# Two paced queues of woven work in the mixers of a two-layer decoder trunk, with four smaller edits

## The chip, the cores and the metric

The kernel runs on one core of a Trainium2 chip. The metric is the device time of one execution in microseconds (us); the time before is the median of 3 runs. The engines are TensorE (PE; its weight loads are PEld), VectorE (DVE), ScalarE (ACT), GpSimd (POOL) and SyncE (SP), which issues the loads.

## The reference

The input is 512 tokens of width 1024, with 16 learned tokens put in front, so 528 columns. There are two layers, and in float32 each layer computes

```python
h = h + rmsnorm(mixer(rmsnorm(h, pre_mix)), post_mix)
h = h + rmsnorm(conv_ffn(rmsnorm(h, pre_ffn)), post_ffn)
```

The mixer is one projection of 1024 to 3600 columns, split into: queries, keys, values and gates of four *retention* heads (rq, rk, rv, rg; 128 wide, rotary on rq and rk, a fixed decay per head); queries, keys, values and gates of four *gated* heads (gq, gk 64 wide, gv, gr 128 wide); and a rank-16 input ga, from which the gated heads' decays come as `log_sigmoid(ga @ w2 + b) / 16`, one per token and key. Retention heads end in a norm with mean and variance, gated heads in a norm with the mean square alone; both are multiplied by silu of their gates, put side by side and sent through one output projection. The second half of a layer is a gated MLP of width 2816 with a causal convolution of three taps between the up-projection and `gelu(a) * g`.

## The kernel before, in words

Activations lie with channels on partitions and tokens along the free dimension. Every large product is done with three float16 matmuls (high x high, low x high, high x low) into one bank: `product_step`, L386 to L388. A weight block of 1024 x 128 is loaded by SP into a stage buffer (st); ScalarE makes its float16 high half (L109), VectorE the low half (L110). The result is a *unit*; there are 10 unit buffers. Tokens are done in two halves (columns 0 to 232 and 232 to 528), so a projection tile is two *half tiles* of 24 matmuls (16 for ga).

**The mixer** (`mixer`, L884) projects 29 tiles in the order of `TILES`. The first LEAD tiles do their first halves, then their second halves, as the second half of the normalised input is not ready before; layer 1 finishes that norm (`self.later`) at this point. All further tiles do both halves in a row. After each half tile comes `tick(2)`, which takes two steps of woven work.

**Woven work** is written as Python generators that yield between steps. `vtr` turns a v tile (2 steps). `gla(pr)` does a pair of gated heads: the decay (`gla_decay`, 3 steps), the diagonal scores (1), eight level steps (`gla_scores`, L833 to L884: each makes a float16 pair lvx with L867 on ScalarE and L868 on VectorE, multiplies k on GpSimd (L870) and q on VectorE (L872), and does the previous level's matmuls lps at L818, merged by predicated copies at L827), the turned k, the states (2), and `head_out`. `ret(h)` does one retention head: scores and turned k (2), states (2), `head_out`. `head_out` (L659) makes the outputs o and o2 in PSUM, one bank each per head; takes statistics on VectorE (L686, L687); forms the reciprocal root with a power on GpSimd (L320); scales into on (L706 for retention, L708 for gated heads); waits until the head's gate is projected; and then, for two token ranges, transposes (pto, L718), multiplies by the gate (L721) and splits into the float16 pair merged (L324, L325). A generator whose gate or v is missing yields "waits" and the next one in the list is tried.

All generators stand in one list, `self.bg`. A step goes to the first that doesn't wait, with `vtr` put at the head of the list, so work runs nearly in series: pair 0 of the gated heads, pair 1, then the retention heads, with the gated heads' last steps when their gates come. Before, all eight gates are the last eight tiles, gr first.

**Order of instructions.** Outside a first region whose order is given by hand, what Python traces is only a ranking. A planner with its own cost model then sets the order on each engine: of the instructions that it believes ready, the earliest traced goes first. `keep_in_program_order` pins an instruction behind everything traced before it on its engine. On the chip each engine works through that fixed order. PSUM has two pools: three banks for projections (`mm`) and five for everything else (`mx`).

**The last stage** (`last_down`, L1133, and `Quarter`, L116) does the last down-projection over quarters of the weight matrix with seven products (w11, t1, t2, w22, t3, w21, t4), five of them on sums of quarters. `Quarter.fetch` traces a load, an addition on VectorE (L143) that adds the landed quarter to one kept, the high half on ScalarE (L154) and the low half on VectorE (L157), up to 8 blocks ahead of use. The loads are pinned, and the high halves of w11 and t1; the additions are not. After w11 and t1, ScalarE copies the sums out (part, L1160) and t2 goes into the same banks. Results (yo, L1168) free banks in which the residual is transposed (hp, L1189).

**The output projection** (`out_proj`, L988) contracts the eight heads in the order 4, 5, 6, 7, 0, 1, 2, 3, where 0 to 3 are retention and 4 to 7 gated heads.

Of the kernel before, what the change touches and what calls it, by code (L numbers as in the profile page):

```python
# [9 lines left out]
F32 = mybir.dt.float32  # L10
# [28 lines left out]
TICK = 2  # L39
# [4 lines left out]
LEAD = (9, 10)  # L44
# [10 lines left out]
TILES += [(nm, 2 * i + j) for i in range(2) for nm in ("rk", "rq", "rv") for j in range(2)]  # L55
TILES += [(nm, h) for nm in ("gr", "rg") for h in range(4)]
# [10 lines left out]
MIXKINDS = (("vnt", P, 6), ("mv", 20, 4), ("bst", 6, 8), ("ms", 10, 4), ("ont", P, 8), ("dgrt", 16, 4), ("dgt", 32, 2))  # L67
# [48 lines left out]
class Quarter:  # L116
# [22 lines left out]
    def fetch(self):  # L139
# [3 lines left out]
        add = lambda to, x: nc.vector.tensor_tensor(out=to, in0=to, in1=x, op=ALU.add)  # L143
# [16 lines left out]
class Kern:  # L160
    def __init__(self, ctx, tc, a):
# [13 lines left out]
        self.rate = 1  # L175
# [6 lines left out]
    def tick(self, n=1):  # L182
        for _ in range(n):
            i = 0
            while i < len(self.bg):
                try:
                    if next(self.bg[i]) is None:
                        break
                    i += 1
                except StopIteration:  # L190
                    self.bg.pop(i)
# [8 lines left out]
    def drain(self):  # L200
        while self.bg:
            self.tick(TICK)

# [171 lines left out]
    def product(self, ps, units, rhs, n0, n1):  # L375

        tot = len(units)
        for i, ((w, kk), x) in enumerate(zip(units, rhs)):
            self.product_step(ps, w, kk, x, n0, n1, i == 0, i == tot - 1)
            if i % 8 == 7 and i + 1 < tot:  # L380
                self.tick(self.rate)
# [277 lines left out]
    def head_out(self, heads):  # L659
# [20 lines left out]
        mv = self.sm([P, n, 5, 2], "mv")  # L680
        nc.gpsimd.memset(mv[:, :, 4, :], 1.0)
        for h in range(n):
            for i in range(5):
                wi = CHUNKS[i][1]
                st = self.sm([P, 6], "bst")
                nc.vector.bn_stats(out=st[:wi], in_=src(h, i))  # L686
                nc.vector.bn_aggr(out=mv[:wi, h, i, :], in_=st[:wi])  # L687
        ret = heads[0][-1] is not None
        if ret:
            r = self.rstd(mv[:, 0, :, 1], 5, 1.0, self.decay[:, 1, heads[0][-1], :])  # L690
# [6 lines left out]
        onvs = []  # L697
        for h in range(n):
            on, ont = self.g([P, 4, P], F32, "on"), self.sm([16, P], "ont")
            onvs.append((on, ont))  # L700
# [584 lines left out]
```

## Time and profile before

| | |
|---|---|
| time, median of 3 runs | 1280.14 us (1280.01 to 1281.91) |
| the profiled execution | 1280.94 us |
| its span, first to last instruction | 1279.2 us |
| mean granted TensorE clock | 0.996 |
| TensorE busy | 1238.6 us (97%) |
| VectorE, ScalarE, GpSimd busy | 827.5, 640.8, 161.5 us |

By the timeline the first mixer runs to about 241 us and the second from 652 to about 878 us; the last stage begins near 1163 us. In a row of groups the columns are: line, engine, operation, what it writes and reads with shapes, count, then busy time and mean ns of one, then the engine's idle time just before and what ended it. Mean ns of a matmul is its latency; matmuls overlap, so the busy time of groups on PE can't be added up. In a row of waits the columns are total us, times and longest. In a timeline row the first two numbers are the start in the span and the duration.

### The profile page before, as it was taken

To read this page: it belongs to the slowest core of one execution; us is meant where nothing else is said; L and a number is where in the kernel's file an instruction comes from. 1 tells how busy PE (TensorE), PEld (TensorE's weight loads), DVE (VectorE), ACT (ScalarE), POOL (GpSimd) and SP (SyncE) were. 2 spreads that over 40 slices of the span, in tenths; PEclk is the share of its full clock that TensorE was granted. 3 is DMA by queue.
4 is the path that set the end of the run, shared out by engine and by line. 5 is a ranking of instruction groups with operands and counts; after the bars stand their busy time and mean duration, and the time that the engine had idled before them with its cause. 6 is when DMAs were issued, how large, how long until landed. Compare 5 with 4: busy or idle time off the path is not lost.

```text
span 1279.2 us, 26402 instructions
## 1 busy us (share of the span) xinstructions
PE 1238.6 (97%) x11106; PEld 1018.2 (80%) x11106; DVE 827.5 (65%) x1518; ACT 640.8 (50%) x1194; POOL 161.5 (13%) x206
## 2 busy tenths in 40 slices
PE   8999999999999999999999898999999999999997
PEld 7877788989888888988887776788898888885443
DVE  5567855467876666422476768454579768887865
ACT  5664443354855555422346544343548656664541
POOL 1013310152000000000330223101530000000000
PEclk9999999999999999999999999999999999999999
DMA  7932212131533323223143321121315333306551
GB/s 208 254 98 68 67 50 83 51 98 35 155 105 95 97 89 91 74 79 97 50 117 96 102 69 51 50 67 50 99 35 159 106 100 100 116 2 201 170 180 66
DMA packets 206828, 124.18 MB, mean 97 GB/s; under 512 B 6689, under 2 KB 194133, under 8 KB 206709
## 3 DMA queue, kind: packets, MB, share of 16 engines
q1 hardware_dynamic: 206548, 121.97, 32.6%
q8 instruction: 87, 1.43, 0.5%
q0 software_dynamic: 160, 0.52, 0.1%
q14 instruction: 33, 0.26, 0.1%
HBM read 120.38 MB, written 2.10 MB: 96 GB/s over the span
## 4 chain that ended last, share of the span: by engine, by line
PE 79%; DVE 9%; ACT 4%; DMA 3%; issue 2%; POOL 2%; SPq 0%; DVEq 0%; POOLq 0%; ACTq 0%
PE pu L387 12%; PE pu L388 12%; PE pu L386 12%; PE pj L386 6%; PE pj L388 6%; PE pj L387 6%; PE pl L1150 3%; PE pd L386 3%; PE pd L388 3%; PE pd L387 3%; DMA st<-in_ffn_down 2%; DVE unit L110 2%; PE po L386 1%; PE po L387 1%; PE po L388 1%
## 5 line engine op out<-in xcount | busy, mean ns | idle before, releaser
L387 PE MATMUL pu<-every,unit 128*128 128x296 f16 (+2 forms) x1408 | 385.4, 274 | 2.1 <-DVE every L325 2.1
L388 PE MATMUL pu<-every,unit 128*128 128x296 f16 (+2 forms) x1408 | 385.4, 274 | 0.0
L386 PE MATMUL pu<-every,unit 128*128 128x296 f16 (+2 forms) x1408 | 383.7, 274 | 0.8 <-ACT every L324 0.7
L110 DVE SCALAR_TENSOR_TENSOR unit<-st,unit 128x1024 f16<-128x1024 f32 x184 | 228.2, 1240 | 162.6 <-ACT unit L109 160.1
L386 PEld LDWEIGHTS <-unit 128*128 128x128 f16 x2912 | 285.4, 98 | 51.0 <-issue 7.0
L388 PEld LDWEIGHTS <-unit 128*128 128x128 f16 x2912 | 285.4, 98 | 46.4 <-issue 3.3
L387 PEld LDWEIGHTS <-unit 128*128 128x128 f16 x2912 | 285.7, 98 | 42.2 <-issue 0.5
L109 ACT ACTIVATE unit<-st 128x1024 f16<-128x1024 f32 x184 | 191.4, 1041 | 134.7 <-PE pu L388 52.7
L386 PE MATMUL pj<-every,unit 128*128 128x296 f16 (+2 forms) x896 | 247.3, 276 | 1.4 <-DVE room L831 1.0
L388 PE MATMUL pj<-every,unit 128*128 128x296 f16 (+2 forms) x896 | 246.8, 276 | 0.7 <-DVE unit L110 0.7
L387 PE MATMUL pj<-every,unit 128*128 128x296 f16 (+2 forms) x896 | 247.3, 276 | 0.0
L1035 ACT ACTIVATE u<-pu 128x296 f32<-128x296 f32 (+2 forms) x176 | 66.3, 379 | 95.9 <-PE pu L388 95.7
L388 PE MATMUL pd<-av,unit 128*128 128x232 f16 (+1 forms) x352 | 96.9, 276 | 0.0
L387 PE MATMUL pd<-av,unit 128*128 128x296 f16 (+1 forms) x352 | 96.8, 276 | 0.0
L386 PE MATMUL pd<-av,unit 128*128 128x232 f16 (+1 forms) x352 | 96.7, 276 | 0.0
L352 DVE TENSOR_TENSOR acc<-acc,sq 128x296 f32<-128x296 f32 (+2 forms) x60 | 33.3, 556 | 75.1 <-ACT sq L350 73.2
L320 POOL TENSOR_TENSOR every<-every 128x1 f32<-128x1 f32 (+5 forms) x33 | 38.8, 1177 | 298.5 <-DVE every L317 124.4
L1150 PE MATMUL pl<-unit,fk 128*128 128x512 f16 x330 | 73.2, 385 | 2.5 <-ACT part L1160 2.5
L386 PE MATMUL po<-merged,unit 128*128 128x296 f16 (+2 forms) x256 | 69.6, 274 | 0.7 <-ACT merged L324 0.7
L387 PE MATMUL po<-merged,unit 128*128 128x296 f16 (+2 forms) x256 | 70.0, 274 | 0.0
L1024 DVE SCALAR_TENSOR_TENSOR cg<-u,every,cg 128x527 f32<-128x527 f32 (+1 forms) x88 | 66.5, 755 | 5.5 <-ACT cg L1019 4.3
L388 PE MATMUL po<-merged,unit 128*128 128x296 f16 (+2 forms) x256 | 70.0, 274 | 0.0
(221 smaller groups left out, 1521.7 us busy)
## 6 DMA issues: line engine op xcount, KB each, us to landing
st<-in_ffn_up SPq DMA_DIRECT2D x88, 512.0 KB, 3.8
st<-in_w_in SPq DMA_DIRECT2D x56, 512.0 KB, 4.1
st<-in_ffn_down SPq DMA_DIRECT2D x46, 512.0 KB, 4.2
st<-in_w_out SPq DMA_DIRECT2D x16, 512.0 KB, 3.5
st<-in_ffn_down SPq DMA_DIRECT2D x8, 384.0 KB, 2.9
out<-yo SPq DMA_DIRECT2D x8, 256.0 KB, 2.0
xt<-in_x SPq DMA_DIRECT2D x6, 256.0 KB, 6.4
w<-in_ffn_down SPq DMA_DIRECT2D x3, 512.0 KB
```

The costliest lines, as they stand in the source:

```text
L109: nc.scalar.activation(u[:, 0], st, AF.Copy, scale=SW)
L110: nc.vector.scalar_tensor_tensor(out=u[:, 1], in0=st, scalar=SW, in1=u[:, 0], op0=ALU.mult, op1=ALU.subtract)
L320: nc.gpsimd.tensor_tensor(out=r[:w, :n], in0=t[:w, :n], in1=self.mhalf[:w, :n], op=ALU.pow)
L352: eng.tensor_tensor(out=acc[:, :n], in0=acc[:, :n], in1=sq[:, :n], op=ALU.add)
L386: nc.tensor.matmul(ps[:, :n], w[:, 0, kk, :], x[:, 0, n0:n1], start=first, stop=False)
L387: nc.tensor.matmul(ps[:, :n], w[:, 0, kk, :], x[:, 1, n0:n1], start=False, stop=False)
L388: nc.tensor.matmul(ps[:, :n], w[:, 1, kk, :], x[:, 0, n0:n1], start=False, stop=last)
L1024: nc.vector.scalar_tensor_tensor(out=to, in0=u[:, max(lo, d) - d : L - d], scalar=self.cvec[:, ci(i) : ci(i) + 1], in1=to, op0=ALU.mult, o ...
L1035: nc.scalar.activation(u[:, n0:n1], ps[:, : n1 - n0], AF.Copy, scale=IXW)
L1150: mm = lambda x, w, **kw: nc.tensor.matmul(ps, x, w, skip_group_check=more, **kw)
```

## The change

1. *Two queues with a pace.* The pairs of gated heads go to a list of their own, `self.gated`; everything else stays in `self.bg`, now strictly in order of arrival (`vtr` no longer at the head). After each half tile `advance` gives each queue one credit (at most one is kept), and takes steps while there is credit. A step costs 0.7; a level step yields `LEVEL / PACE[0]` and so costs 1.5. `tick` is left for the other stages, with one step a call as they had it.
2. *Tiles.* The gates gr 0 and gr 1 come right after the first two retention heads' tiles, gr 2 and gr 3 last of all. The leading tiles of layer 1 are nine where they were ten.
3. *Norms of gated heads.* ScalarE squares each output chunk with a running sum and later scales it; the statistics, the square of the mean and the scaling on VectorE go for these heads. Retention heads keep theirs.
4. *Output projection.* Heads are contracted in the order 0, 1, 4, 5, 2, 3, 6, 7.
5. *Last stage.* The additions of `Quarter.fetch` are pinned in program order.

```diff
-TICK = 2
+PACE = (0.7, 0.7)
+LEVEL = 1.5
-LEAD = (9, 10)
+LEAD = (9, 9)
-TILES += [(nm, 2 * i + j) for i in range(2) for nm in ("rk", "rq", "rv") for j in range(2)]
-TILES += [(nm, h) for nm in ("gr", "rg") for h in range(4)]
+TILES += [(nm, j) for nm in ("rk", "rq", "rv") for j in range(2)] + [("gr", 0), ("gr", 1)]
+TILES += [(nm, j) for nm in ("rk", "rq", "rv") for j in range(2, 4)] + [("rg", h) for h in range(4)] + [("gr", 2), ("gr", 3)]
...
-        add = lambda to, x: nc.vector.tensor_tensor(out=to, in0=to, in1=x, op=ALU.add)
+        add = lambda to, x: kern.tc.keep_in_program_order(nc.vector.tensor_tensor(out=to, in0=to, in1=x, op=ALU.add))
...
+    def step(self, queue):
+        i = 0
+        while i < len(queue):
+            try:
+                n = next(queue[i])
+                if n != "waits":
+                    return n or 1.0
+                i += 1
+            except StopIteration:
+                queue.pop(i)
+        return 0
+    def tick(self):
+        self.step(self.bg)
+    def advance(self):
+        for i, queue in enumerate((self.gated, self.bg)):
+            self.credit[i] = min(self.credit[i] + 1.0, 1.0)
+            while self.credit[i] > 0:
+                n = self.step(queue)
+                if not n:
+                    break
+                self.credit[i] -= n * PACE[i]
...
     def drain(self):
-        while self.bg:
-            self.tick(TICK)
+        while self.bg or self.gated:
+            for queue in (self.gated, self.bg):
+                self.step(queue)
...
         yield
-        mv = self.sm([P, n, 5, 2], "mv")
...
+        ret = heads[0][-1] is not None
+        onvs = [(self.g([P, 4, P], F32, "on"), self.sm([16, P], "ont")) for _ in heads]
+        if ret:
...
         else:
             q = self.sm([P, n, 5], "ms")
-            nc.vector.tensor_tensor(out=q, in0=mv[:, :, :, 0], in1=mv[:, :, :, 0], op=ALU.mult)
-            nc.vector.tensor_tensor(out=q, in0=q, in1=mv[:, :, :, 1], op=ALU.add)
-            r = self.rstd(q.rearrange("p h i -> p (h i)"), 5 * n, 1.0, EPS * 64.0)
-        yield
+            nc.gpsimd.memset(q[:, :, 4], 1.0)
+            for h, i, wi in each:
+                nc.scalar.activation(to(h, i), src(h, i), AF.Square, accum_out=q[:wi, h, i : i + 1])
+            r = self.rstd(q.rearrange("p h i -> p (h i)"), 5 * n, 1.0 / P, EPS * 64.0)
+        yield
...
+                nc.scalar.activation(to(h, i), src(h, i), AF.Copy, scale=rr)
...
-            yield
+            yield LEVEL / PACE[0]
...
-                self.spawn(gla(0))
-                self.spawn(gla(1))
+                self.gated.extend([gla(0), gla(1)])
             elif nm in ("gv", "rv"):
-                self.bg.insert(0, vtr((nm, h)))
+                self.spawn(vtr((nm, h)))
...
-            self.tick(TICK)
-        self.rate = 1
+            self.advance()
...
-        order = [4, 5, 6, 7, 0, 1, 2, 3]
+        order = [0, 1, 4, 5, 2, 3, 6, 7]
```

More of the change, by code (lines that the diff above doesn't have):

```diff
@@ L174, in __init__ @@
         self.bg = []
-        self.rate = 1
+        self.gated, self.credit = [], [0.0, 0.0]
         self.rings = {}
@@ L180, in spawn @@
         self.bg.append(gen)
[L182 to L191, printed above, removed]
+    def step(self, queue):
[19 more added lines that the diff above has]
+                self.credit[i] -= n * PACE[i]
     def finish(self, gen):
@@ L380, in product @@
             if i % 8 == 7 and i + 1 < tot:
[L381 removed]
+                self.tick()
     def product_step(self, ps, w, kk, x, n0, n1, first, last):
@@ L679, in head_out @@
         yield
-        mv = self.sm([P, n, 5, 2], "mv")
[L681 to L684, printed above, removed]
+        ret = heads[0][-1] is not None
+        onvs = [(self.g([P, 4, P], F32, "on"), self.sm([16, P], "ont")) for _ in heads]
+        to = lambda h, i: onvs[h][0][:, i, :] if i < 4 else onvs[h][1]
+        each = [(h, i, CHUNKS[i][1]) for h in range(n) for i in range(5)]
+        if ret:
+            mv = self.sm([P, 5, 2], "mv")
+            nc.gpsimd.memset(mv[:, 4, :], 1.0)
+            for h, i, wi in each:
@@ L685, in head_out @@
                 st = self.sm([P, 6], "bst")
                 nc.vector.bn_stats(out=st[:wi], in_=src(h, i))
[L687 to L690, printed above, removed]
+                nc.vector.bn_aggr(out=mv[:wi, i, :], in_=st[:wi])
+            r = self.rstd(mv[:, :, 1], 5, 1.0, self.decay[:, 1, heads[0][-1], :])
         else:
             q = self.sm([P, n, 5], "ms")
-            nc.vector.tensor_tensor(out=q, in0=mv[:, :, :, 0], in1=mv[:, :, :, 0], op=ALU.mult)
-            nc.vector.tensor_tensor(out=q, in0=q, in1=mv[:, :, :, 1], op=ALU.add)
-            r = self.rstd(q.rearrange("p h i -> p (h i)"), 5 * n, 1.0, EPS * 64.0)
+            nc.gpsimd.memset(q[:, :, 4], 1.0)
@@ L696, in head_out @@
+            for h, i, wi in each:
+                nc.scalar.activation(to(h, i), src(h, i), AF.Square, accum_out=q[:wi, h, i : i + 1])
+            r = self.rstd(q.rearrange("p h i -> p (h i)"), 5 * n, 1.0 / P, EPS * 64.0)
         yield
[L697 to L700, printed above, removed]
-            for i in range(5):
-                wi = CHUNKS[i][1]
-                to = on[:, i, :] if i < 4 else ont
-                rr = r[:wi, 5 * h + i : 5 * h + i + 1]
-                if ret:
-                    nc.vector.tensor_scalar(out=to, in0=src(h, i), scalar1=mv[:wi, h, i, 0:1], scalar2=rr, op0=ALU.subtract, op1=ALU.mult)
-                else:
-                    nc.vector.tensor_scalar(out=to, in0=src(h, i), scalar1=rr, scalar2=None, op0=ALU.mult)
+        for h, i, wi in each:
+            rr = r[:wi, 5 * h + i : 5 * h + i + 1]
+            if ret:
+                nc.vector.tensor_scalar(out=to(h, i), in0=src(h, i), scalar1=mv[:wi, i, 0:1], scalar2=rr, op0=ALU.subtract, op1=ALU.mult)
+            else:
+                nc.scalar.activation(to(h, i), src(h, i), AF.Copy, scale=rr)
```

4 lines of the change are left out of this document (1 added, 3 removed).

## The prediction

> **What bounds the kernel now.** I read the page first, then the busy time by stretch, then the list of waits.
>
> ```profile
> PE 1238.6 (97%) x11106; PEld 1018.2 (80%) x11106; DVE 827.5 (65%) x1518; ACT 640.8 (50%) x1194; POOL 161.5 (13%) x206
> ```
>
> TensorE works for 1238.6 of 1279.2 us, and the change takes no matmul away. What can be won is its idle time, 40.6 us, and time at a lowered clock. Some of the idle time is the start and the last 7 us, which the change doesn't touch. So the question is how much lies in the two mixers. By stretch (span, then PE, PEld, DVE, ACT and POOL busy, clock, DMA):
>
> ```profile
> 75.00:155.00 80.00, 74.63 (x967) 59.10 (x965) 65.83 (x168) 39.90 (x77) 26.14 (x28) 1.00 0.24 69
> 710.00:812.00 102.00, 90.10 (x1083) 70.89 (x1082) 77.78 (x211) 44.40 (x86) 29.20 (x38) 0.98 0.22 63
> 155.00:245.00 90.00, 89.77 (x780) 77.75 (x779) 50.63 (x154) 36.22 (x84) 9.97 (x10) 1.00 0.22 64
> ```
>
> The reader is to see that the idle time has a place. In 75 to 155 and 710 to 812, where the gated heads' level scores are worked, PE loses 5.4 and 11.9 us, and VectorE is busy 82% and 76% of the time. In 155 to 245, where the retention heads run, PE loses 0.2 us. This row also gives the cost of a projection matmul: 89.77 us for 780 is 115 ns, so a half tile of 24 takes 2.8 us.
>
> ```profile
> PE lps L818 <- ACT lvx L867: 9.3, 14, 1.6
> PE lps L818 <- DVE lvx L868: 2.9, 3, 1.2
> PE pl L1150 <- ACT part L1160: 2.5, 1, 2.5
> ...
> PE pto L718 <- DVE on L706: 1.5, 1, 1.5
> PE hp L1189 <- DVE yo L1168: 1.3, 1, 1.3
> PE rst L743 <- DVE on L708: 1.1, 1, 1.1
> PE ptv L637 <- ACT room L646: 1.0, 1, 1.0
> ```
>
> These are waits of PE over the whole span. The level scores (lps) wait 12.2 us for their split operand (lvx). Three more lie in the last stage and at the mixer's end (pl, pto, hp: 5.3 us). The last two rows are matmuls that waited for a bank of the five-bank pool to be read out.
>
> **Part 1: the pace.** One level is a chain: ACT makes the high half, VectorE the low half, GpSimd multiplies k, and the next level starts.
>
> ```profile
> L867 ACT ACTIVATE lvx<-room 128x528 f16<-128x528 f32 x16 | 11.5, 717 | 25.2 <-DVE room L872 12.4 <-DVE room L853 5.1 <-DVE tots L875 4.0
> ```
>
> ```profile
> L868 DVE TENSOR_TENSOR lvx<-room,lvx 128x528 f16<-128x528 f32 x16 | 11.8, 736 | 2.3 <-ACT lvx L867 2.0
> ```
>
> ```profile
> L870 POOL TENSOR_TENSOR room<-room,tots 128x264 f32<-128x264 f32 x12 | 10.6, 883 | 13.1 <-DVE lvx L868 10.9 <-DVE tots L875 2.1
> ```
>
> ```profile
> L818 PE MATMUL lps<-lvx x192: 162/190/200, 84.3 to 108.5; 64*128 64x64 f16 x168, 64*16 64x8 f16 x24
> ```
>
> ```profile
> 88.30 0.20 PE L818 MATMUL lps<-lvx 64*128 64x64 f16 x2 [1.41 <-ACT lvx L867]
> ```
>
> Alone the chain takes 0.72 + 0.74 + 0.88 = 2.3 us; as it ran, seven levels from 84.3 to 108.5, one level took 24.2 / 6 = 4.0 us, since the three engines do other work between. The code before asks for two steps after each half tile, a level in 1.4 us of projections. That can't be kept, so the planner fills PE with later projections and puts each lps where its own costs say that lvx is just ready. There is no slack, and where the chip is later than the planner thinks, PE stands (the 1.41 us at 88.30). After the change a level is charged 1.5 half tiles, 4.1 us of projections, with lps and the second queue's matmuls on top: by working the two queues through by hand, the first pair's levels fall after half tiles 15 to 26 of the sequence (before: 19 to 22) and the second pair's after 36 to 47 (before: 28 to 33): 24 half tiles have a level among them instead of 10. The pace asked, 4.1 us plus the woven rest, is at or above the 4.0 us that the chain took, so lps comes up in PE's order after lvx is done.
>
> Removed: of the 17.3 us idle in the two stretches, those that end on lvx (12.2) and most of what goes with them. Bounds: 0 (the planner still leaves no slack) to 17.3. I take 13.0, three quarters, as the pace clears the chain by little and VectorE, at 82%, still is the fullest engine behind PE there.
>
> **Part 2: the gated norms on ScalarE.** For a pair of heads VectorE's 10 statistics, 10 aggregates, 2 small operations and 10 scalings go, and ScalarE gets 10 squares with a sum and 10 scaled copies.
>
> ```profile
> L686 DVE BATCH_NORM_STATS2 room<-o x10: 253/278/299, 115.8 to 118.1; 128x6 f32<-128x128 f32 x8, 16x6 f32<-16x128 f32 x2
> L708 DVE TENSOR_SCALAR on<-o,every x8: 329/335/350, 121.3 to 123.3; 128x128 f32<-128x128 f32 x8
> ```
>
> ```profile
> L645 ACT ACTIVATE vn<-ptv,every 128x128 f32<-128x128 f32 x32 | 9.0, 364 | 7.2 <-PE ptv L637 7.2
> L758 ACT ACTIVATE sn<-kv 128x128 f32<-128x128 f32 x32 | 8.9, 277 | 26.4 <-PE kv L757 26.0
> ...
> L905 ACT ACT_TABLE_LOAD x2 | 2.6, 1283 | 0.0
> ...
> L1170 ACT ACTIVATION_READ_ACCUMULATOR sqo<-yo 128x1 f32 x6 | 1.1, 186 | 0.0
> ```
>
> ```profile
> L320 POOL TENSOR_TENSOR every<-every 128x10 f32<-128x10 f32 x4 | 7.9, 1965 | 0.5
> ```
>
> No row shows a square of 128x128 with a sum; nearest are a PSUM copy (277 ns) and the read of a sum (186 ns): 10 x 0.46 = 4.6 us, and 10 copies with a scale per partition at 0.36 = 3.6 us. ScalarE gets 8.2 us a pair, 33 us in all, and goes from 641 to 674 us, 53% of the span; VectorE loses some 6 us a pair. Neither lies on PE's path while projections run. What does: a pair's four o banks of the pool of five. Now they are held from 115.8 (first statistic) to about 123.7, 8 us; after, 4.6 + 2.0 (the power on GpSimd) + 3.6 and two hand-overs make 10 to 11 us. Who waits behind: the transposes of v, scores and outputs of the retention queue, each wanting one or two banks, and now issued beside the gated queue rather than after it. Bounds: 0 (three projection banks cover 3 x 2.8 = 8.4 us) to 4 pairs x 2.5 = 10 us. I take +2.5, as the two rows of bank waits above are 1 us each.
>
> The gates gr 0 and gr 1 come between the two pairs' exponentials (a, L801), so the Silu table is loaded, the exponential's again, and Silu again: two more loads a mixer, 4 x 1.28 = 5.1 us on ScalarE, beside half-idle time. The Trainium skill's "ScalarE: Activation LUTs", under "Rules for kernel authors", speaks against this: do all of one table set before switching. By its figure of 2.66 us a switch, drain included, the four would be 10.6 us; by the row they are 5.1, and on PE's path nothing by either while ScalarE is half idle.
>
> **Part 3: nine leading tiles, the gates' place, the order of the output projection.** In layer 1 the second halves start one half tile sooner, but their input comes from a chain of its own:
>
> ```profile
> 673.94 0.82 PE L546 MATMUL nbc<-ndg,every 99*128 99x99 f32 x6
> ```
>
> ```profile
> 674.79 1.82 DVE L559 SCALAR_TENSOR_TENSOR tmp<-every,nbc 128x296 f32<-128x296 f32 x4 [2.33 <-PE nbc L546]
> ```
>
> The first operand of the second half appears only after 674.8. If PE arrives a half tile, 2.8 us, earlier it can stand up to 2.8 us, or nothing if the planner draws the tenth tile's first half forward. I take +0.7.
>
> At the end of a mixer the output projection now contracts heads in the order in which they come ready. Before, layer 1 ended with PE waiting 1.5 us for the last retention norm (pto above), and then came these steps:
>
> ```profile
> 888.07 0.40 DVE tmp L721
> 888.55 0.42 ACT merged L324
> ```
>
> After, by the same hand count, what is left for the end is one step of the second gated pair, its norm done five half tiles before. After the last gate: Silu, product, high and low half, four steps of some 0.4 us by these rows, 1.7 us, lie under 7 heads x 3 matmuls x 0.115 = 2.4 us. So the 1.5 us go in layer 1. Bounds 0 and -1.5; I take -1.5, since its cause, the late norm, is gone.
>
> **Part 4: ordered sums.** In the last stage VectorE adds landing weight quarters (L143), and ScalarE (L154) makes their high halves:
>
> ```profile
> 1173.42 1.23 DVE L143 TENSOR_TENSOR w<-w,st 128x1024 f32<-128x1024 f32 x1 [1.76 <-DMA st<-in_ffn_down]
> ...
> 1179.10 2.35 DVE L143 TENSOR_TENSOR every<-every,st 128x1024 f32<-128x1024 f32 x2
> ```
>
> ```profile
> 1193.03 2.03 ACT L1160 ACTIVATE part<-pl 128x512 f32<-128x512 f32 x4
> ```
>
> The sums on w at 1173.42 and after belong to the next product (t2), the one at 1179.10 to the product that is running (t1, quarter 8), whose data was asked for first. t1's high halves keep their order on ScalarE, so t2's queue up behind them, and the copy of the first sums (part) comes at 1193.03; PE stands 2.5 us for it. With sums in program order t1's come first, the high halves start some 6 us sooner (1179.1 - 1173.4), and ScalarE is free when PE is done. SP's loads stand in the same order and wait for the buffers that the sums give back, so they come no later. Likewise the sums of the last product (t4) now follow the results that free the banks for hp: 1.3 us. Bounds: a gain of 3.8; a loss of 2.4, if a sum of t4 and its low half, 1.2 us each, now come late for PE, since an ordered sum that waits for its DMA holds all of VectorE behind it. I take -3.0, near the two rows of waits.
>
> **Part 5: the clock.** The stretches before and in each fall of the clock:
>
> ```profile
> 784.00:788.00 4.00, 1.59 (x51) 1.17 (x51) 4.00 (x11) 1.26 (x3) 0.67 (x2) 1.00 0.44 131
> 788.00:792.00 4.00, 4.00 (x20) 2.34 (x17) 2.58 (x5) 1.35 (x4) 2.26 (x4) 0.57 0.00 0
> ...
> 1190.00:1194.00 4.00, 1.53 (x8) 0.63 (x7) 4.00 (x5) 4.00 (x7) 0.00 (x0) 1.00 0.46 161
> 1194.00:1198.00 4.00, 4.00 (x13) 1.47 (x11) 3.01 (x4) 1.92 (x4) 0.00 (x0) 0.57 0.00 0
> ```
>
> Twice, right after PE had been idle for 2.4 to 2.5 of 4 us, the granted clock was 0.57 over 4 us, which costs 0.43 x 4 = 1.7 us. Both stalls are ones that parts 1 and 4 should end. Bounds 0 to -3.4; I take -1.7, as other stretches may now be the idle ones. The Trainium skill's "TensorE: Matmul & The Clock Gate", under "HAM oscillation", has the clock fall after gaps over about 3.4 us. By that rule these shorter waits would not be the cause, nothing would be won here, and the sum below would end at 1266.6. The trace's waits are 2.5 us at most, so it doesn't agree.
>
> **The sum.** -13.0 + 2.5 + 0.7 - 1.5 - 3.0 - 1.7 = -16.0 us. The profiled execution took 1280.94 us, 1279.2 of it span and 1.7 around it, and lies 0.8 above the median of 1280.14: 1280.94 - 16.0 = 1264.9 us, which I forecast as 1265. With the best bounds (-17.3, 0, 0, -1.5, -3.8, -3.4) it is 1255; with the worst (0, +10, +2.8, 0, +2.4, 0) 1296.
>
> **The rivals.**
>
> *The planner leaves no slack at any pace.* Then the waits on lvx stay and move with the levels; of the sum 13.0 go, and half of the clock's 1.7: -2.2, so 1278.8. For it: the planner ranks by its own costs, and these costs stay as they are. Against it: 155 to 245, where the same planner weaves at the same two steps a half tile with shorter chains, has 0.2 us of idle time.
>
> *The banks become the bound, and the kernel slower.* Two queues now want the five-bank pool at once. By the hand count the first gated pair's outputs (four banks) and those of retention head 0 (two) are issued after the same half tile, 29; the second pair's share half tile 50 with the transposes of the last v. Where such a matmul stands next in PE's order, the three projection banks are no cover, and PE waits for what is left of 10.5 us. It decides from the point where the wait exceeds some 2.5 us at two matmuls for each of the four pairs: at that price 8 x 2.5 = 20 in place of the 2.5 taken, and as late retention work pushes the levels, half of the 13.0 goes: -16.0 + 17.5 + 6.5 = +8.0, so 1289. For it: rst and ptv already waited for banks. Against it: four banks are held for 8 us now too, and cost 1 us.
>
> *The second gated pair comes late.* Its queue has little to spare: 8 levels at 1.5 and 13 steps at 0.7 make 21.1 half tiles a pair, 42.2 of the 45 there are. If it lags by the three half tiles that lie between its norm and the end beyond the 10.5 us, each output projection waits for the norm instead of for a gate. At 4 us a mixer, and without the 1.5 of part 3: -16.0 + 1.5 + 8.0 = -6.5, so 1274. For it: level chains run late by nature. Against it: VectorE is relieved just there.
>
> **How the numbers follow.** The forecast has 0.60, no slack 0.14, the banks 0.15, the late pair 0.11. Anything within 0.2% (2.6 us, 1277.6 to 1282.7) can't be told from no change here. Faster: nearly all of the first, most of the late pair and a third of the no-slack case, 0.72; no change: mostly no slack, 0.10; slower: the banks and the rest, 0.18. The forecast's own range is 1255 to 1273 (the better bounds, and half of the worse ones); for 8 in 10 it reaches on to the late pair and the no-slack case and leaves most of the banks' out: 1254 to 1284, the lower end 1 us under the best bounds for the idle time that has no row.
>
> **What would show it.** Right: waits of lps on lvx under 4 us in all where they were 12.2; PE idle in the two mixers' level stretches under 6 us; no wait for part, and none of pto in layer 1; ScalarE near 674 us with four more table loads; no 0.57 stretch in the second mixer. Wrong: new rows of PE waiting for on, vn or sn (banks), long waits before po (late pair), or lps rows as before (no slack).

## The result and the profile after

The changed kernel took 1273.3 us (median of 4 runs, 1272.95 to 1275.55) against 1281.03 us for the kernel before on the same chip: a ratio of 0.9943, with a 95% interval of 0.9926 to 0.996. That is 7.7 us faster. The forecast was 1265 us, 16.0 us faster. The sign was right and under half of the size came.

The profiled execution took 1275.55 us, with a span of 1273.8 us (before: 1279.2). Its page has this row:

```profile
PE 1239.0 (97%) x11106; PEld 1022.0 (80%) x11106; DVE 802.6 (63%) x1390; ACT 666.4 (52%) x1318; POOL 163.0 (13%) x206
```

TensorE's idle time fell from 40.6 to 34.8 us; its busy time did not fall. By stage (span, then PE, PEld, DVE, ACT and POOL busy, granted clock, DMA), before and then after; the stretches are the first mixer, its output projection, the second mixer, its output projection, and the last stage. The two feed-forward parts left out are as long as they were.

```profile
0.00:241.50 241.50, 231.55 (x2279) 193.68 (x2279) 153.80 (x387) 122.09 (x250) 41.78 (x56) 1.00 0.40 114
241.50:288.30 46.80, 45.93 (x408) 39.68 (x407) 25.60 (x45) 22.35 (x51) 21.88 (x23) 1.00 0.28 80
...
651.70:877.70 226.00, 213.53 (x2167) 177.76 (x2167) 146.81 (x371) 106.51 (x223) 44.05 (x59) 0.99 0.27 78
877.70:927.50 49.80, 47.40 (x419) 40.13 (x419) 23.92 (x53) 21.91 (x52) 19.51 (x23) 1.00 0.26 75
...
1162.50:1279.20 116.70, 105.64 (x496) 49.04 (x494) 80.68 (x96) 44.84 (x63) 3.25 (x6) 0.97 0.51 167
```

```profile
0.00:239.50 239.50, 230.30 (x2262) 193.72 (x2263) 138.03 (x307) 132.55 (x304) 39.40 (x56) 0.99 0.40 115
239.50:290.90 51.40, 48.65 (x424) 41.43 (x423) 29.30 (x61) 24.78 (x57) 22.04 (x23) 1.00 0.25 72
...
654.40:876.70 222.30, 214.27 (x2161) 179.47 (x2161) 130.88 (x299) 116.21 (x279) 46.05 (x56) 0.97 0.28 79
876.70:927.10 50.40, 47.72 (x425) 40.60 (x424) 26.61 (x61) 24.37 (x57) 19.71 (x24) 1.00 0.25 74
...
1162.10:1273.80 111.70, 103.40 (x496) 48.81 (x494) 81.05 (x96) 45.26 (x63) 4.75 (x6) 0.98 0.51 174
```

Added up per layer, the first mixer with its output projection became 2.6 us longer (288.3 to 290.9), the second 3.1 us shorter (275.8 to 272.7), the last stage 5.0 us shorter. The first mixer alone ended 2.0 us sooner; its output projection, which now also holds 424 matmuls where it had 408, took 4.6 us more.

The waits of PE after (total us, times, longest):

```profile
PE lps L831 <- ACT lvx L880: 3.6, 2, 1.9
PE rs L755 <- POOL rq L746: 2.8, 2, 1.8
PE pto L731 <- DVE on L719: 2.7, 2, 1.4
PE pu L404 <- DVE every L342: 2.1, 4, 0.6
PE ptv L654 <- ACT gv L918: 2.0, 1, 2.0
...
PE pj L403 <- DVE on L719: 1.7, 2, 0.9
PE po L403 <- DVE tmp L734: 1.5, 2, 0.9
```

The 12.2 us on lvx are 3.6 now, and part and hp are gone. In their place stand waits that are new or longer: the retention scores (rs) for the rope's sum on GpSimd and a value tile's transposes (ptv) for that tile's own copy out of its bank are new; the last transposes (pto) now wait for a retention head's norm in both mixers, where they waited in one; and po waits for the merged product (tmp).

The second part is the clock. In the trace the granted clock is either full or half, and half in stretches of 3.413 us or twice that. Before there were two such stretches ahead of the last matmul, at 788.2 and 1194.4 us (6.8 us at half clock). After there are five windows, at 170.6, 655.3, 706.5 and two from 805.5 (17.1 us). Windows of the kernel after, each dip with the window ahead of it:

```profile
167.20:170.60 3.40, 1.66 (x37) 1.35 (x37) 3.40 (x8) 1.57 (x4) 1.59 (x2) 1.00 0.01 2
170.60:174.00 3.40, 3.40 (x16) 2.11 (x15) 3.28 (x9) 0.09 (x1) 1.92 (x2) 0.50 0.53 154
```

```profile
651.90:655.30 3.40, 1.19 (x10) 0.74 (x9) 3.39 (x8) 2.63 (x7) 0.34 (x8) 1.00 0.42 120
655.30:658.70 3.40, 3.35 (x18) 2.56 (x18) 3.40 (x11) 1.74 (x5) 0.00 (x0) 0.50 1.14 309
703.10:706.50 3.40, 1.35 (x16) 0.98 (x16) 1.50 (x2) 3.37 (x7) 0.00 (x0) 1.00 0.48 139
706.50:709.90 3.40, 3.40 (x23) 2.06 (x22) 2.56 (x6) 0.62 (x3) 0.00 (x0) 0.50 0.71 201
802.10:805.50 3.40, 1.53 (x37) 0.88 (x34) 3.40 (x7) 2.25 (x4) 3.08 (x3) 1.00 0.00 0
805.50:812.30 6.80, 5.05 (x22) 3.25 (x21) 4.66 (x13) 0.64 (x1) 4.47 (x5) 0.50 0.27 80
```

Ahead of each fall PE was busy for 1.19 to 1.66 us of a window, 35 to 49%. If a half-clock window cost half its length, the clock's share would have gone from 3.4 to 8.5 us in these two profiled executions, 5.1 us against the change. The timed executions give a smaller price and a smaller share. The kernel after, with its repeat below, had eight: the four at a mean clock of 0.996 took 1272.95 to 1273.2 us, the three at 0.992 took 1274.9 to 1275.55, so about 2.3 us for a difference of some three windows. Over all kernels measured here, a mean clock lower by 0.001 goes with about 0.7 us from one execution of a kernel to the next; a half-clock window takes off 0.0013, so it costs some 0.9 us by this estimate. And the kernel before had a mean clock of 0.9948 in the 52 executions that were timed beside the experiments, the kernel after 0.9943: of the difference of their medians the clock carries about 0.4 us, not 5.1. The experiments test the waits and the clock.

### The profile page after: what moved, and what is told of

The parts are those of the page before. It is cut to its first block, busy times and chain, and to the rows that moved or that the text cites. A ratio compares the mean times of both kernels' runs of the same rounds, so it can differ in the third digit from the quotient of the medians.

```text
span 1273.8 us, 26361 instructions
## 1 busy us (share of the span) xinstructions
PE 1239.0 (97%) x11106; PEld 1022.0 (80%) x11106; DVE 802.6 (63%) x1390; ACT 666.4 (52%) x1318; POOL 163.0 (13%) x206
## 4 chain that ended last, share of the span: by engine, by line
PE 82%; DVE 5%; ACT 4%; issue 4%; POOL 2%; DMA 1%; SPq 1%; POOLq 0%; DVEq 0%; ACTq 0%
PE pu L404 12%; PE pu L405 12%; PE pu L403 12%; PE pl L1160 8%; PE pj L403 6%; PE pj L405 6%; PE pj L404 6%; PE pd L403 3%; PE pd L405 3%; PE pd L404 3%; DVE unit L111 1%; PE po L404 1%; PE po L405 1%; ACT unit L110 1%; PE po L403 1%
## 5 line engine op out<-in xcount | busy, mean ns | idle before, releaser
L337 POOL TENSOR_TENSOR every<-every 128x1 f32<-128x1 f32 (+5 forms) x33 | 41.4, 1256 | 326.3 <-DVE every L336 235.1
```

Source lines behind the costliest of these rows:

```text
L337: nc.gpsimd.tensor_tensor(out=r[:w, :n], in0=t[:w, :n], in1=self.mhalf[:w, :n], op=ALU.pow)
```

## The experiments

Medians are compared with the kernel before as timed beside them on the same chip (1280.1, 1279.9, 1279.6 and 1281.0 us). The kernel after had 1273.3 and, repeated, 1273.95; "1273.6" in the expectations is their mean.

### The last stage and the mixers, each alone

The first kernel is the one before with `add` pinned, the second the one after with `add` free.

```diff
-        add = lambda to, x: nc.vector.tensor_tensor(out=to, in0=to, in1=x, op=ALU.add)
+        add = lambda to, x: kern.tc.keep_in_program_order(nc.vector.tensor_tensor(out=to, in0=to, in1=x, op=ALU.add))
```

> The kernel before with the one edit of the last stage alone: the adds of the sums stay in program order. My theory after the two traces: the last stage became 5.0 us shorter by this edit alone, 3.3 us of it the waits that went (part, hp) and 1.7 us the half-clock stretch at 1194 us that followed such a wait. So about 1281.0 - 5.0 = 1276.0 us (1275 to 1278), and the last stage shows no wait of TensorE on part or hp. Rival: the half-clock stretch is chance and the idle time comes back elsewhere; then not over 1.7 us are gained, 1279.3 us or more.

> The kernel after without the ordered sums, so with all that was changed in the mixers. My theory: the mixers are worth 7.7 - 5.0 = 2.7 us, since the 8.6 us that the waits on lvx lose are taken back by new stalls (ret scores behind the rope sum on GpSimd, values behind gv, merged tiles at the end) and by more half-clock stretches: 1278.3 us (1277 to 1280). Rival: the sums are worth 1.7 us or less, and the mixers 6: 1275 us.

Measured: sums alone 1279.15 us (ratio 0.9991, 0.9979 to 1.0002), mixers alone 1274.67 us (0.9952, 0.9938 to 0.9966). My attribution fell: the mixers carry some 5.4 us and the sums about 1, which the interval of the sums alone does not tell from nothing. The last stage of each, sums alone and then mixers alone:

```profile
1164.00:1275.70 111.70, 103.36 (x496) 48.78 (x493) 81.13 (x96) 45.25 (x63) 4.71 (x6) 0.98 0.51 174
```

```profile
1159.30:1272.90 113.60, 103.68 (x495) 48.67 (x493) 80.78 (x95) 44.73 (x63) 3.16 (x6) 0.99 0.51 172
```

With pinned sums the stage is 111.7 us, as in the kernel after; with free sums and no fall of the clock it is 113.6, though PE waits there for part as before. So the sums are worth 1.9 us beside this run, not the 5.0 that the two first profiles showed: 1.7 of those were a half-clock window (1194.4) that free sums don't always bring, and the kernel before had waited longer on hp (1.3 us against 0.4). In the run with the sums alone, half-clock windows stood elsewhere (722.5, 787.4, 889.8), and its 12 times spread from 1276.5 to 1282.8 us in step with the granted clock, 0.997 to 0.991: a straight line through them gives 0.85 us for each 0.001.

### The pace alone, in the one list of before

```diff
             if step > 0:
                 self.level_scores(step - 1, xs.pop(step - 1), dg, dt)
             yield
+            yield
```

> The kernel before with one edit: after each of the eight levels of a gated pair one step of the woven work is left empty, so the one list of before takes one level per half tile instead of two, and everything behind it in the list comes 16 steps later per mixer. My theory: TensorE's waits on lvx fall from 12.2 us to under 5, as in the kernel after; but two retention heads, some 18 steps, are left for the drain behind the last half tile, where nothing covers them, at about 1 us of TensorE idle a step: 2 x 18 x 1 = 36 us more less 8, so about 1309 us (1290 to 1330). So the pace alone can't be had with one list. Rival: what drains is covered or cheap, and the pace alone gives the gain: 1271 to 1276 us.

Measured 1305.73 us (1.0196, 1.018 to 1.0211), as expected. The waits:

```profile
PE pto L718 <- DVE on L706: 17.5, 7, 2.7
PE lps L818 <- DVE lvx L868: 3.3, 6, 0.9
PE pl L1151 <- ACT part L1161: 2.4, 1, 2.4
PE lps L818 <- ACT lvx L867: 2.3, 2, 1.6
```

lvx costs 5.6 us instead of 12.2, so the pace does what it says; but the retention heads left for the drain (the woven steps that are worked off behind the last half tile) cost 17.5 us on pto alone. PE's idle time rose by 9.5 us in all and its busy time by 15.8 us, with 41 us at half clock where there were 6.8. In one list, this pace costs more than it saves.

### One level per half tile

```diff
-LEVEL = 1.5
+LEVEL = 1.0
```

> The kernel after with a level's cost 1.0 instead of 1.5: each half tile gets one level instead of two in three. My theory: a level's chain on ScalarE, VectorE and GpSimd takes longer than one half tile where ropes run beside it, and about that where not, so TensorE's waits on lvx rise from 3.6 us to 5 to 10 us and the time to 1276 us (1274.5 to 1279). Rival: one level a half tile is slow enough; the waits stay under 4 us, and since the second pair ends eight half tiles earlier the time falls by 1 us or more, to 1272.6 us or less.

Measured 1275.88 us (0.9965, 0.9952 to 0.9977), and 5.9 us of waits on lvx (3.8 on ScalarE, 2.1 on VectorE). So one level per half tile already takes away half of the 12.2 us, and the slower pace 2.3 us more. The times agree in sign, 2.3 us, though their intervals overlap.

### The kernel after, profiled again

> The kernel after as it is, in a second profiled execution. My theory: the clock is decided on a fixed grid of 3.413 us that runs free of the kernel, and a window in which TensorE was busy less than about half is followed by one at half clock; so the stalls stand at the same places within 1 us of the span with the same lengths, but the half-clock stretches differ in place or number from the five inside the span of the first profile (170.6, 655.3, 706.5, and two windows at 805.5). Rival: the stretches follow from the stalls alone; then the same five windows stand at the same stalls. The time is 1273.3 us either way (1272.9 to 1275.6).

The unchanged kernel had 1273.95 us. My expectation missed in the profile: the same five windows stood at half clock, as the grid lay the same, within 0.1 us, in both executions. The timed executions did differ: 1273.0 us at a clock of 0.996 twice, 1274.9 and 1275.5 at 0.992. A repeat of another kernel, below, shows the grid at work.

### The second list's pace, and later starts

```diff
-PACE = (0.7, 0.7)
+PACE = (0.7, 0.5)
```

> The kernel after with one number changed: the second list's pace is 0.5 instead of 0.7, so two steps of a retention head are issued per half tile instead of 1.43. My theory: in the kernel after the last two retention heads stand one behind the other in that list, and head 3's scaled tiles are ready only when its transposes are next, so TensorE waits at the end of both mixers for them (1.47 and 1.56 us) and around it (0.64 and 0.98 us). At 0.5 they are issued three half tiles earlier: these four go, 4.7 us of TensorE's waits, and the time is 1273.6 - 4 = 1269.6 us (1268.5 to 1271.5). Rival: the wait at the end is the last gate's own way (Silu, merge, split) and not the list; then the waits on pto stay and the time is 1273 to 1275 us.

Measured 1271.96 us (0.9939, 0.9926 to 0.9953). The waits on pto are gone, so the second list had been their cause; but the gain is 1.6 us and not 4. New waits came:

```profile
PE rs L755 <- POOL rq L746: 3.3, 3, 2.2
PE d L861 <- DVE on L719: 3.2, 2, 1.6
...
PE ptv L654 <- ACT gv L918: 2.0, 1, 2.0
```

They are not the whole reason, as PE's idle time fell all the same, from 34.8 to 29.2 us. PE's busy time rose by 2.0 us with one half-clock window fewer, and why is open; the five executions had a mean clock of 0.992, against 0.994 for the kernel after. Then, on top of it, later starts:

```diff
         def ret(hd):
             res = {}
+            yield 1.01 / PACE[1]
             yield from self.ret_scores(out["rk", hd], out["rq", hd], res)
...
         def vtr(key):
-            yield
+            yield 1.01 / PACE[1]
```

> The same, and besides a retention head's scores and the turning of a values' tile begin one half tile later (a step left empty at their head). My theory: the waits of TensorE on the rope's sum on GpSimd (rs, 1.24 and 1.94 us) and on gv (ptv, 2.2 us in the second mixer) come from issuing these steps behind the same half tile that makes their input; they go, and with them the half-clock stretches at 706 and 805 us: 5.4 us of waits and up to 5 us at half clock less in the second mixer. Time 1266 us (1264 to 1269). Rival: the steps that come later meet the end of the mixer, where nothing covers them, and the time is that of the run without it, 1270 us, or more.

Measured 1264.61 us (0.988, 0.9867 to 0.9894), 9 us below the kernel after. The time came out as expected, the rows only in part: the wait on rs is gone in the first mixer, but still 1.8 us in the second, and ptv has 1.7; against the kernel after, pto fell from 2.7 to 0.8 us, and three of the five half-clock windows went. On the other side lvx has 3.3 us, where the run at 0.5 had 0.9, and projections (pj) wait 2.5 us for a retention head's scaling on VectorE (L719). So the step from 1272 to 1264.6 us does not stand in the waits. The pages of the run at 0.5 and of this one:

```profile
PE 1241.0 (98%) x11106; PEld 1023.1 (81%) x11106; DVE 805.3 (63%) x1390; ACT 665.5 (52%) x1318; POOL 158.9 (13%) x206
```

```profile
PE 1232.0 (98%) x11106; PEld 1019.6 (81%) x11106; DVE 801.7 (63%) x1390; ACT 666.6 (53%) x1318; POOL 163.4 (13%) x206
```

The span fell by 7.4 us (1270.1 to 1262.7), PE's idle time rose by 1.4 us, and its busy time fell by 9.0. Two half-clock windows fewer make at most 3.4 of that; what made the rest, with the same 11106 matmuls, is open. Against the kernel after, 11.1 us of span are 4.2 us of idle time and 7.0 us of busy time.

That one half tile of 2.8 us isn't enough for rs in the second mixer fits what GpSimd does in the kernel after, where two sums of a rope take 3.8 us:

```profile
804.21 3.79 POOL L746 TENSOR_TENSOR rq<-rq,tmp 128x218 f32<-128x218 f32 x2 [0.32 <-DVE tmp L745]
```

### The same kernel twice

> The run with the later starts a second time, beside the three others on one chip. Theory: 1264.6 us again within 1 us, by which the step of 9 us from the kernel after stands. Rival: the first was a lucky draw of the clock's grid; then 1266 to 1269 us.

Measured 1265.47 us (0.988, 0.9865 to 0.9894): the step stands. The profiled execution had a span of 1265.6 us, the first 1262.7, with the same waits of PE (lps 3.3, rs 1.8, ptv 1.7 us in both) but four half-clock windows ahead of the last matmul instead of two. The stall around ptv in the first execution and in the second:

```profile
698.80:702.20 3.40, 1.98 (x16) 1.63 (x17) 2.28 (x2) 2.62 (x5) 0.00 (x0) 1.00 0.28 84
702.20:705.60 3.40, 3.40 (x30) 2.77 (x29) 3.09 (x9) 1.23 (x2) 0.00 (x0) 1.00 0.98 277
```

```profile
698.10:701.50 3.40, 1.74 (x18) 1.24 (x17) 1.42 (x2) 3.37 (x6) 0.00 (x0) 1.00 0.51 143
701.50:704.90 3.40, 3.40 (x16) 2.10 (x14) 3.37 (x8) 0.45 (x2) 0.00 (x0) 0.50 0.70 188
```

One program, one wait of 1.7 us: in the first execution the grid cuts it so that the window is 58% busy, and the clock stays; in the second the window is 51% busy, and it falls. Two windows more, 2.9 us more span: 1.45 us a window by this pair, of which 0.3 us is idle time.

### A filled stall

In the kernel after, four matmuls of ones go into the bank of the second mixer's first projection, which then overwrites them. They run while TensorE waits for the scaled columns.

```diff
+FILL = 4
...
+        if half == 0:
+            for _ in range(FILL):
+                nc.tensor.matmul(ps[:, :P], self.ones, self.ones, start=True, stop=True)
```

> The kernel after with four more matmuls of ones, whose result is overwritten and used by nobody, in the stall of 1.9 us at the start of the second mixer (TensorE waits there for the scaled columns). My theory: it is the busy share of TensorE in a window of the 3.413-us grid that decides, not the work's progress; filled, no window there is under half busy at any phase, so the half-clock stretch at 655 us doesn't come, and nothing is slower by the fill: 1273.6 less the 1.3 us of one window, 1272.3 us (1271.3 to 1274). Rival: the clock goes down for another reason, for instance by what follows; then the stretch stands there as before, and the time is 1273.6 us or later by what the fill overlaps, up to 1274.5 us.

Measured 1271.6 us (0.9929, 0.9915 to 0.9943), 2.0 us below 1273.6; the intervals overlap, so the rows decide. The window with the stall and the one behind it:

```profile
652.70:656.10 3.40, 2.03 (x19) 1.68 (x18) 3.39 (x8) 2.80 (x7) 0.34 (x8) 1.00 0.71 200
656.10:659.50 3.40, 3.40 (x38) 3.35 (x37) 3.27 (x11) 1.53 (x4) 0.05 (x1) 1.00 1.19 294
```

Sixty per cent busy, and the clock stays full where it had fallen at 655.3. The grid also lay otherwise in this execution, so one profile alone proves little: in the run with the mixers alone the stall, not filled, fell into a window 54% busy (653.2 us), and the clock stayed full too. With the repeat above the run agrees with the busy share as the cause; it doesn't show that the fill brought the 2.0 us.

### Ten leading tiles

```diff
-LEAD = (9, 9)
+LEAD = (9, 10)
```

> The kernel after with ten leading tiles in the second mixer, as before. My theory: with nine the mixer's second halves begin 0.8 us too early for their norm, one stall of 0.82 us at 681 us; with ten it goes and the rest moves by one half tile: 1272.8 us (1271.5 to 1274), which the interval hardly tells from 1273.6. Rival: the ninth tile was chosen for the rest of the mixer, and with ten the second list runs later against the end: 1274.5 us or more.

Measured 1269.97 us (0.9918, 0.9905 to 0.9931): 3.6 us, not 0.8. The stall at 681 us (0.9 us with the short wait ahead of it) is gone, and from 654 to 877 us the kernel after had four windows at half clock, this run one there and one behind it. With half of each window's length taken out, the second mixer would be as long as it was (215.9 against 215.5 us). But the four executions had a mean clock of 0.9958 against 0.9943, which is some 1 us by the 0.7 us for 0.001, and PE's idle time fell by 2.3 us (34.8 to 32.5); so the clock is a part of the 3.6 us, and how much isn't settled.

### The gated heads' norms back on VectorE

The norm of the gated heads in `head_out` is the code of before again; first on the kernel after, then on the run with later starts.

> The kernel after with the gated heads' norms back on VectorE (mean and variance, as in the kernel before). My forecast had put ScalarE's norms at +2.5 us, by four more table loads and banks held longer; by that the time is 1271 us. My theory now: the profile after shows no wait of TensorE on the gated heads' banks, so the move is worth nothing or a little: 1273.6 us within 1.5, with VectorE 25 us busier and ScalarE about 26 us less. Rival: VectorE's time is what holds the levels, and the undo costs 3 us or more, 1276.5 us, with longer waits on lvx.

> The run with the later starts (second list at 0.5, scores and values one half tile later: 1264.6 us) and the gated heads' norms back on VectorE. My theory: ScalarE's norms cost about 2.7 us, as forecast, since on the kernel after their undo gave 1273.6 to 1270.9; the two add up: 1262 us (1260.5 to 1263.5). Rival: the undo had removed waits that the later starts remove as well, or moved the grid of the clock; then it is 1264 to 1266 us.

On the kernel after: 1270.92 us (0.9929, 0.9917 to 0.9941), 2.7 us faster, the very sum that my forecast had against ScalarE. On the later starts: 1270.8 us (0.9925, 0.9912 to 0.9938), 6 us slower. So the norms have no price of their own. On the kernel after, PE's waits on lvx fell with the undo from 3.6 to 0.6 us and those on pto from 2.7 to none, while waits of po for a gate came:

```profile
PE po L403 <- ACT gr L917: 3.6, 2, 2.1
...
PE lps L830 <- ACT lvx L879: 0.6, 1, 0.6
```

ScalarE makes the high half of lvx, and with less to do there it is hardly late for the levels. With the later starts the last retention head's statistics fall, by the hand count, beside the second gated pair's, and with both on VectorE pto has 2.7 us where it had 0.8, and the wait on vn is new, while lvx fell from 3.3 to 2.3. Whether that meeting is the cause was not tried:

```profile
PE pto L730 <- DVE on L718: 2.7, 2, 1.5
PE lps L830 <- ACT lvx L879: 2.3, 2, 1.7
PE kv L769 <- ACT vn L662: 2.1, 2, 1.4
```

### The last two tiles in order

The kernel after weaves the last two result tiles: by its instruction order their 33 matmuls each are issued in turns of 1 to 12, where the kernel before did one tile and then the other. So two chains of Square, sum, power and scaling stand behind the last matmul. Of the last scalings, before and then after:

```profile
1274.47 1.41 DVE L1178 SCALAR_TENSOR_TENSOR yo<-yo,every,hp 128x512 f32<-128x512 f32 x2 [0.72 <-POOL every L320]
```

```profile
1266.93 1.40 DVE L1188 SCALAR_TENSOR_TENSOR yo<-yo,every,hp 128x512 f32<-128x512 f32 x2
...
1269.11 1.41 DVE L1188 SCALAR_TENSOR_TENSOR yo<-yo,every,hp 128x512 f32<-128x512 f32 x2 [0.72 <-POOL every L337]
```

The edit pins the matmuls of t4.

```diff
...
+                                if what == "t4":
+                                    self.tc.keep_in_program_order(one)
```

> The kernel after with the matmuls of the very last product (w22's high half, two tiles of 33) kept in program order: first tile whole, then the second, as they stood before. My theory: the ordered sums took 3.1 us of waits out of the last stage and gave 1.2 us back behind the last matmul, because with them the two last tiles came to be woven into one another, so both ends' chains (Square, sum, power, scale, store) stand behind the last matmul: 8.7 us from the last matmul's start to the end of the span, against 7.5 before. In order it is 7.5 us again, and the time 1273.6 - 1.2 = 1272.4 us (1271.5 to 1273). Rival: the end is set by the store alone; then 8.7 stays and the time is 1273.6 us.

Measured 1280.83 us (1.0009, 0.9998 to 1.0019), 7 us slower. I had seen the end and not the middle:

```profile
PE hp L1202 <- DVE yo L1191: 3.4, 1, 3.4
...
PE hp L1202 <- DVE yo L1181: 2.4, 1, 2.4
```

Pinned, PE stands 5.8 us for banks that the residual's transposes need, with two half-clock windows; the woven order covers that with the other tile.

### Combinations

Everything that had seemed to help at once (later starts, norms back, ten leading tiles, pinned last tiles):

> All that helped together: second list at 0.5, later starts, norms back on VectorE, ten leading tiles in the second mixer, last tiles in order. My theory, by the sum: 1262 less 1.2 at the end and 0.7 for the stall at the lead: 1260 us (1258.5 to 1262). Rival: they hide one another and the time is 1262 to 1265 us.

Measured 1276.02 us (0.9967, 0.9954 to 0.998); two of its parts do harm, by the runs above. Later starts with ten leading tiles, and the same with the filled stall:

> The run with the later starts (second list at 0.5, scores and values one half tile later, norms on ScalarE: 1264.6 us) and ten leading tiles in the second mixer. My theory: the 0.7-us stall at the lead goes, and one half-clock window at 801 us may go with the shift: 1263.5 us (1262 to 1265). Rival: as with the norms, a shift by one half tile brings new waits; 1266 to 1270 us.

> The run before this one in the list, later starts with ten leading tiles, and the four matmuls in the stall at the start of the second mixer. My theory: the stretch at 651 us goes, 1.3 us less than without the fill: 1262 us (1260.5 to 1264). Rival: no difference that can be told, or slower.

Measured 1268.03 us (0.99, 0.9884 to 0.9916) and 1266.69 us (0.9891, 0.9878 to 0.9905), against 1265.47 for the later starts alone beside them. Ten leading tiles, worth 3.6 us on the kernel after, are worth nothing here: a new wait for the last retention norm (2.6 us) empties a window there, and two half-clock windows follow it, from 869 us. With the filled stall the clock again stayed full behind it; the median is 1.3 us lower, within the intervals. The best kernel found is the one with the later starts, 15 us below the kernel before.

## Why the prediction was right and wrong

**Part 1, the pace: right in mechanism, too large by a third, and wrong in what it left out.** The groups of lps, before and after (busy, mean ns, idle before them):

```profile
L818 PE MATMUL lps<-lvx 64*128 64x64 f16 (+1 forms) x768 | 22.2, 188 | 12.8 <-ACT lvx L867 9.3 <-DVE lvx L868 2.9 <-DVE room L831 0.4
```

```profile
L831 PE MATMUL lps<-lvx 64*128 64x64 f16 (+1 forms) x768 | 19.2, 187 | 3.7 <-ACT lvx L880 3.6
```

Idle time ahead of lps fell by 9.1 us where I took 13.0. (The group's busy time fell by 3.0 us as well, but matmuls overlap, and PE's busy time in all did not fall.) Between the first and the last lps of each pair PE is idle for 6.6 us in all, just over the 6 that I had named, and the two long waits that stay are at the second pair's first levels. The step that failed is the silence about new waits: the sum has no term for a step that waits for an input made beside it. Working the queues by hand, I had the half tile of each level and each norm, and did not ask of every step whether its input was made in that same half tile. It was, for the retention scores (rs 2.8 us) and for a value tile (ptv 2.0); and the retention heads, one behind the other in a list at 0.7, were late at the end (pto 2.7, po 1.5), where I took -1.5 for part 3. Against what stood there before (pto 1.5, rst 1.1, ptv 1.0) these four rows, with the wait of pj for a retention head's scaling (1.7), are 10.7 us, 7.1 us more: more than half of part 1. With this the idle time adds up, the small rows left aside: 9.1 us less on lvx and 3.8 less on part and hp, 7.1 more in new waits, make the 5.8 us by which it fell (40.6 to 34.8), where the terms of the forecast without the clock make 14.3. The runs show part of the cause of these waits: a second list at 0.5 took away pto and po, and later starts took rs from the first mixer, but not from the second, and hardly changed ptv. That the two edits together reach 1264.6 to 1265.5 us, where the forecast stood, does not prove the term, as most of that step is not idle time.

**Part 5, the clock: -1.7 was forecast, and it gave nothing.** In the two profiled executions there are five windows where there were two; over the timed executions the mean clock hardly moved (0.9948 to 0.9943, some 0.4 us the wrong way). That falls follow stalls was right; that the change would leave fewer of them was wrong, as the waits of 1.7 to 2.1 us that stood after (on lvx, on gv and on the rope's sum) emptied windows too. The price of half a window's length, 1.7 us, was too high as well: the runs show 0.9 to 1.45 us. So of the 8 us that were missed in the medians, the clock is about 2, and the new waits, with the 3.9 us that lvx fell short of 13.0, are the larger part.

**Part 4, the ordered sums: right that part and hp end** (no such rows after), over-sized in time. I had -3.0; the stage shows -1.9 beside the mixers alone, and the medians about -1 (the sums alone -2.7 to +0.3 by the interval). The step missed was that a new order on VectorE lets the planner change PE's order too: the last two tiles came to be woven.

**Part 2, the norms: forecast +2.5, measured +2.7 on this kernel, mostly by another way.** ScalarE came to 666.4 us where 674 was forecast, with four more table loads (14 against 10) as said. The first pair's banks were held for 11.8 us (126.4 to 138.2) where I had 10 to 11, as ScalarE did a table load and other work between the squares; but of waits that may be for banks only 0.8 us went with the undo (pj, 1.7 to 0.9). The larger part is ScalarE's lateness for lvx, 3.0 us, which I had put at nothing because ScalarE is half idle on average. So the close number is luck, and it holds for this order alone: on the later starts its sign is the other.

**Part 3: +0.7 for nine tiles was the stall of 0.9 us seen at 681 us**; the undo gave 3.6 us, in part by the clock. The -1.5 for the end of layer 1 did not come: pto waits 1.4 us there for a retention head's norm. The early place of two gates and the new order of the heads were not tried on their own.

**The sum and the rivals.** The sum started from the profiled execution, 1280.94 us, though the median that it forecasts was 1280.14; from there it ends at 1264.1 us, a difference too small to matter. The time fell on the third one's 1274, but not by its mechanism: what came late at the end was a retention head, not the second gated pair. Of the second there are at most single waits of 0.9 us (pj, behind a retention head's scaling), far from its price. The no-slack case is refuted by 3.6 us on lvx.

## What to carry to other kernels

When work is moved to another place in a weave, write down for each step in which slot its inputs are made, and give it a slot of distance, or more where its input takes longer than a slot; a step that becomes issuable in the slot that feeds it can stall the engine. Price a stall on TensorE at its length plus, when it may empty about half of a clock window, some 1 to 1.5 us. Take the clock's share from the timed executions, not from one profile. Then look at busy time as well as waits: here the largest step of an experiment stood in no wait. And measure an edit on the kernel that it will stay in: the norms and the tenth tile changed their worth by 9 and 6 us with the order around them.

## What the runs showed of the hardware

The granted clock goes by a grid of 3.413 us. In each trace the starts of all half-clock stretches have the same remainder by 3.413 us, within 0.01 us, and between traces that remainder lay anywhere from 0.77 to 3.36 us. Over all the traces, of the windows at full clock between the first 8 us and the last matmul, all 35 that were under 42% busy were followed by a half-clock one, of 48 between 42 and 57% 26 were, and of some 6450 above that only two (the share counts a matmul's latency, so it is no exact measure of work). Stalls of 1.7 us are enough when they fall inside one window: the same 1.7-us stall ahead of the second mixer brought a fall after a window 35% busy (after) and none after one 52% busy (before):

```profile
648.20:651.60 3.40, 1.78 (x15) 1.36 (x14) 3.18 (x6) 1.75 (x5) 0.29 (x6) 1.00 0.16 20
651.60:655.00 3.40, 2.76 (x27) 2.55 (x27) 3.40 (x10) 1.94 (x7) 0.00 (x0) 1.00 0.94 292
```

The Trainium skill's "TensorE: Matmul & The Clock Gate", under "What's actually happening", has a free-running window of 3413 ns; the traces agree. Its rule under "HAM oscillation", that gaps must stay under about 3.4 us, is too lenient for this kernel: the longest wait of PE in the kernel after is 2.0 us, and five windows fell.

One program's time varies with its mean clock by some 2 to 3 us from one execution to the next (1272.95 to 1275.55 us for the kernel after), which is as much as most single edits here are worth.
